# Seven modulation vectors: from dot products on VectorE to column-group matmuls on TensorE

## The chip, the core and the metric

The kernel runs on one core of a Trainium2 chip. The metric is device time in microseconds (us) of one execution, taken as the median of several; smaller is better. The engines that matter here are PE (TensorE, the matrix engine), DVE (VectorE), ACT (ScalarE), POOL (GpSimd) and SP (the queue that issues most of the DMAs). Each works through its own instructions in a fixed order.

## The reference, cut to what matters

A two-layer model handles 256 prompt tokens and 1024 sample tokens. Each layer has a mixer and an MLP, and each of these is modulated by six vectors of 1024 numbers per layer, made from a conditioning vector (one for the prompt, one for the sample):

```python
def _modulation(cvec, w, b):            # cvec (., 1024), w (1024, 6144), b (6144,)
    m = jax.nn.silu(cvec) @ w + b
    return jnp.split(m[:, None, :], N_MOD, axis=-1)

for l in range(DEPTH):                  # DEPTH = 2
    mp = _modulation(c_ctx[None, :], mod_w[l], mod_b[l])
    ms = _modulation(c, mod_w[l], mod_b[l])
    hp = _rmsnorm(xp, norm_mix[l]) * (1.0 + mp[1]) + mp[0]
    ...                                 # mixer; x = x + m[2] * mixer
    hp = _rmsnorm(xp, norm_mlp[l]) * (1.0 + mp[4]) + mp[3]
    xp = xp + mp[5] * _mlp(hp, mlp_w1[l], mlp_w2[l])
    ...                                 # the same for the sample stream with ms
```

Everything is float32. The MLP is `square(relu(h @ w1)) @ w2` with 4096 hidden units.

## The kernel before, in words

The activations stand as 8 tiles of 128 channels by 1280 tokens (`NT`). A float32 product is made of three matmuls on rounded halves (`fp32r`: high by high, high by low, low by high).

The program goes through filter preparation, the even mixer with attention, a first MLP, the odd mixer (Hyena and FNet), and a second MLP. It is written as a Python trace. The instructions of each engine are then put in order by a planner that runs through the trace with durations of its own (`schedule_with_timeline_sim=True`): what stands earlier in the program goes first where it is ready, and later work fills in. Tiles come from pools with a fixed number of buffers; a tile that finds no free buffer waits for the release of an earlier one.

`mlp` (L786 on) has two stages. Its first stage (`w1`) runs 16 turns (`for j in range(16)`), each of seven products of 24 matmuls in `product` (L846; two turns are begun ahead). The weights come by `wraw` (a DMA into `wr`, L811), `wset` (sums on POOL, L821 and the `sub` helper L300, through a temporary `s1`) and `wtile` (a rounding copy on ACT, L805, and a subtraction on DVE or POOL, L300). DVE and ACT take the products out of PSUM (L857, L860, L921 to L929), DVE squares the rectified results (L927, L930) and SP stores them (L928, L931). The second stage (`w2`) has its matmuls at L1034 and starts with PSUM reopened, after `drain(filler)`.

At the end of each turn `pull(filler, 4)` advances a generator by four steps. In the second MLP that generator is empty. In the first MLP it is `fill2`, which computes seven of the twelve modulation vectors: layer 0's sixth, and all six of layer 1. It does so with `modulation(l, which)`: for each vector, two halves of the input dimension and eight output chunks, a weight tile `mt` of 128 outputs by 512 inputs (256 KB) is loaded (L380), and for each of the two conditioning vectors DVE multiplies it with a broadcast copy `cb` of silu(c) and sums along the row (L382). `cb` comes from DRAM (`cscr`), written there by `silu_rows` between the two filter transforms. Partial sums lie in `macc` and are added up at L388 and L389.

The other five vectors (all of layer 0 but the sixth) are made by `modulation_pe`, three at the start and two inside attention: the conditioning vector stands as stationary weights (`silu`, 32 columns, two of them used), the weight tile `mw` streams 256 columns, and four input chunks go to four column groups of PE, so that each lands in 32 partitions of its own in one PSUM bank (L357). ACT copies the bank to `ms` (L362), and eight small matmuls with the selection matrix `sel` (L368) add the four groups and turn the result; DVE adds the bias (L369).

The temporaries `mt`, `mj`, `ms`, `s1` and several others share one pool (`tp`, tag `t`) of 4 buffers of 128 by 512 floats. `silu` takes one of the 24 large slots of pool `gp` (tag `g`) until attention is through. `tbank` gives one of two PSUM banks.

Of the kernel before, what the change touches and what calls it, by code (L numbers as in the profile page):

```python
# [8 lines left out]
F32 = mybir.dt.float32  # L9
F32R = mybir.dt.float32r  # L10
AF = mybir.ActivationFunctionType
ALU = mybir.AluOpType
# [131 lines left out]
def _pack(i):  # L144
    def A(x):
        return np.asarray(x)

    o = {}
# [3 lines left out]
    o["crow"] = np.stack([A(i["c_ctx"]), A(i["c"])[0]])  # L152
    mw = A(i["mod_w"])
    o["mw"] = mw[0, :, :5120].reshape(2, 4, 128, 20, 256).transpose(3, 0, 2, 1, 4).reshape(20, 2, 128, 1024)
    o["mt"] = mw.reshape(2, 2, 512, 6, 4, 2, 128).transpose(0, 3, 1, 4, 6, 5, 2).reshape(2, 6, 2, 4, 128, 1024)
# [40 lines left out]
    for t, n in enumerate(("lru_w_r", "lru_w_i")):  # L196
        w = A(i[n])[0]
# [26 lines left out]
def build(tc, a, out, dbg=None):  # L224
# [6 lines left out]
    tp = root.enter_context(tc.tile_pool(name="tp", bufs=4))  # L231
# [13 lines left out]
    def slot(name, shape, dt=F32, tag="g"):  # L245
        return gp.tile(shape, dt, tag=tag, name=name, bufs=SLOTS if tag == "g" else HSLOTS)

    def tmp(name, shape=(128, 512)):
        return tp.tile(list(shape), F32, tag="t", name=name)
# [9 lines left out]
    def tbank():  # L259
        return psum["t"].tile([128, 512], F32, tag="t", name="pt")  # L260
# [28 lines left out]
    cscr = dp.tile([2, 1024], F32, name="cscr")  # L289
# [29 lines left out]
    st = slot("silu", [128, 8, 32])  # L319
    mod = [[cp.tile([128, 8, 2], F32, name=f"mod{l}{i}") for i in range(6)] for l in range(2)]  # L320
    macc = cp.tile([128, 6, 2, 8, 2], F32, name="macc")
# [5 lines left out]

    def silu_rows():
        crow = slot("crow", [2, 1024])
        csg = slot("csg", [2, 1024])  # L330
        ld(crow, a["crow"])
        S.activation(csg, crow, AF.Sigmoid)
        V.tensor_tensor(csg, csg, crow, ALU.mult)
        ld(cscr, csg)

    def modulation_pe(i, bk=tbank, tags=("wr",)):
        mss = []
        for jj in range(2):
            ws = []
            for n in range(4):  # L340
# [5 lines left out]
                (ld if len(tags) == 1 else LDM)(w.rearrange("p k c -> p (k c)"), a["mw"][4 * i + 2 * jj + h, kk])  # L346
# [25 lines left out]
    def modulation(l, which):  # L372
        for hf in range(2):
            cb = cp.tile([128, 2, 512], F32, tag="cb", name="cb")
            for s_ in range(2):
                ld(cb[:, s_], cscr[s_:s_ + 1, 512 * hf:512 * hf + 512].to_broadcast([128, 512]))
            for i in which:
                for c in range(8):
                    w, j = tmp("mt"), tmp("mj")
                    ld(w, a["mt"][l, i, hf, c // 2, :, 512 * (c % 2):512 * (c % 2) + 512])  # L380
                    for s_ in range(2):
                        V.scalar_tensor_tensor(j if s_ == 0 else w, w, 1.0, cb[:, s_], ALU.mult, ALU.mult,  # L382
                                               accum_out=macc[:, i, hf, c, s_:s_ + 1])
                    if c % 2:
                        yield
        for i in which:
            m = mod[l][i]
            V.tensor_tensor(m, macc[:, i, 0], macc[:, i, 1], ALU.add)  # L388
            V.tensor_tensor(m, m, mb[:, l, 8 * i:8 * i + 8].unsqueeze(2).to_broadcast([128, 8, 2]), ALU.add)  # L389
        yield  # L390
# [1507 lines left out]
    # ================= program =================  # L1898
    with root:
# [74 lines left out]
        silu_rows()  # L1974
# [98 lines left out]
```

## Time and profile before

| | us |
|---|---|
| three runs: median (lowest to highest) | 3344.59 (3343.64 to 3347.43) |
| profiled execution, span from first to last instruction | 3345.9 |
| PE busy with matmuls in the span | 2960.5 (88%) |
| DVE busy | 2512.5 (75%) |
| POOL busy | 1406.4 (42%) |
| ACT busy | 1225.1 (37%) |

The page gives the span of the profiled execution and no other time of it; it lies 1.3 us above the median of the runs and inside their spread. A float32 matmul (not rounded halves) is recorded as two MATMUL instructions: L357 has 96 calls for three vectors and 192 records.

In the rows below, a group of instructions is given as line, engine, operation, output<-input, shapes, count, then busy time and mean duration, then the engine's idle time just before and what ended it. A timeline row is start, length, engine, line, operation and count, with the idle time before it in brackets. A wait row is who waited, for whom, total, times and longest.

### The profile page before, as it was taken

To read this page: it belongs to the slowest core of one execution; us is meant where nothing else is said; L and a number is where in the kernel's file an instruction comes from. 1 tells how busy PE (TensorE), PEld (TensorE's weight loads), DVE (VectorE), ACT (ScalarE), POOL (GpSimd) and SP (SyncE) were. 2 spreads that over 40 slices of the span, in tenths; PEclk is the share of its full clock that TensorE was granted. 3 is DMA by queue.
4 is the path that set the end of the run, shared out by engine and by line. 5 is a ranking of instruction groups with operands and counts; after the bars stand their busy time and mean duration, and the time that the engine had idled before them with its cause. 6 is when DMAs were issued, how large, how long until landed. Compare 5 with 4: busy or idle time off the path is not lost. (4 is left out here: it accounts for less than half of the span.)

```text
span 3345.9 us, 46730 instructions
## 1 busy us (share of the span) xinstructions
PE 2960.5 (88%) x18190; PEld 2716.9 (81%) x18190; DVE 2512.5 (75%) x3172; ACT 1225.1 (37%) x2032; POOL 1406.4 (42%) x912
## 2 busy tenths in 40 slices
PE   6799978897999998989799998887979999899977
PEld 3577767796988887989778876777979999898976
DVE  6886798648999987887983257875686656788896
ACT  5556757634111125333233332322432222533322
POOL 3530054524433336555630025543244344555563
PEclk8899989998999998999899998898989999999988
DMA  6363232341445443132331235546212223323232
GB/s 237 115 235 111 99 126 81 128 163 60 167 161 167 161 167 111 64 101 70 101 139 37 82 121 176 182 145 208 101 70 86 102 97 125 109 70 97 68 131 95
DMA packets 133336, 407.03 MB, mean 122 GB/s; under 512 B 14886, under 2 KB 29622, under 8 KB 133116
## 3 DMA queue, kind: packets, MB, share of 16 engines
q1 hardware_dynamic: 121596, 362.10, 31.6%
q0 software_dynamic: 11520, 41.95, 4.2%
q8 instruction: 144, 2.36, 0.3%
q14 instruction: 76, 0.62, 0.1%
HBM read 306.70 MB, written 97.29 MB: 121 GB/s over the span
## 5 line engine op out<-in xcount | busy, mean ns | idle before, releaser
L846 PE MATMUL pd<-BT,wt 128*128 128x320 f32 x3072 | 474.9, 314 | 42.5 <-ACT BT L764 21.6
L805 ACT CAST wt<-wr 128x512 fp32r<-128x512 f32 x360 | 221.2, 620 | 770.3 <-PE pd L1034 233.3
L846 PEld LDWEIGHTS pd<-BT,wt 128*128 128x128 f32 x3072 | 463.5, 192 | 48.1 <-ACT BT L764 22.6
L1034 PE MATMUL pd<-oT,wt 128*128 128x320 f32 x2688 | 427.8, 318 | 64.5 <-DVE acc L1040 54.5
L1034 PEld LDWEIGHTS pd<-oT,wt 128*128 128x128 f32 x2688 | 413.3, 195 | 72.7 <-issue 31.1
L846 PE MATMUL pd<-B,wt 128*128 128x320 f32 x2304 | 364.0, 315 | 35.2 <-DVE u L926 14.9
L846 PEld LDWEIGHTS pd<-B,wt 128*128 128x128 f32 x2304 | 349.4, 192 | 41.5 <-ACT wt L805 16.9
L1034 PE MATMUL pd<-o,wt 128*128 128x320 f32 x2016 | 324.7, 319 | 42.5 <-DVE acc L1040 25.8
L1034 PEld LDWEIGHTS pd<-o,wt 128*128 128x128 f32 x2016 | 310.5, 196 | 51.5 <-issue 24.6
L1040 DVE TENSOR_TENSOR acc<-acc,pd 128x640 f32<-128x640 f32 x336 | 270.2, 812 | 84.1 <-PE pd L1034 83.9
L300 DVE TENSOR_TENSOR wt<-wr,wt 128x512 fp32r<-128x512 f32 x276 | 265.8, 965 | 61.7 <-ACT wt L805 61.6
L923 POOL TENSOR_TENSOR u<-ut,u 128x640 f32<-128x640 f32 x32 | 55.0, 1719 | 413.0 <-ACT u L922 277.2
L300 POOL TENSOR_TENSOR ur<-ur 128x640 f32<-128x640 f32 x84 | 165.3, 1979 | 111.7 <-DVE o L300 69.5
L300 POOL TENSOR_TENSOR wt<-wr,wt 128x512 fp32r<-128x512 f32 x84 | 133.6, 1590 | 164.3 <-ACT wt L805 164.3
L300 POOL TENSOR_TENSOR wr<-wr 128x512 f32<-128x512 f32 x120 | 196.9, 1641 | 8.0
L692 PE MATMUL pb<-hh,wl 128*128 128x258 f32 (+1 forms) x720 | 191.9, 369 | 0.0
L692 PE MATMUL pb<-hh,wh 128*128 128x258 f32 (+1 forms) x720 | 191.5, 368 | 0.5 <-ACT hh L643 0.3
L692 PE MATMUL pb<-hl,wh 128*128 128x258 f32 (+1 forms) x720 | 191.5, 367 | 0.0
L303 ACT CAST wh<-wr 128x1024 fp32r<-128x1024 f32 x74 | 77.5, 1048 | 195.8 <-PE pd L692 79.8
L725 POOL TENSOR_TENSOR nacc<-nacc,nsq 128x640 f32<-128x640 f32 (+2 forms) x36 | 60.3, 1675 | 210.2 <-ACT nsq L724 210.1
L692 PEld LDWEIGHTS pb<-hh,wh 128*128 128x128 f32 x720 | 121.9, 190 | 27.9 <-issue 6.5
L692 PEld LDWEIGHTS pb<-hh,wl 128*128 128x128 f32 x720 | 121.9, 191 | 25.8 <-issue 6.0
(536 smaller groups left out, 6419.2 us busy)
## 6 DMA issues: line engine op xcount, KB each, us to landing
wr<-in_w_dram SPq DMA_DIRECT2D x136, 512.0 KB, 3.6
uscr<-u SPq DMA_DIRECT2D x64, 640.0 KB, 3.3
ur<-uscr SPq DMA_DIRECT2D x64, 640.0 KB, 4.9
tab<-in_dft_dram POOLq DMA_DIRECT2D x79, 512.0 KB, 4.7
mt<-in_mt_dram SPq DMA_DIRECT2D x112, 256.0 KB, 3.0
mw<-in_mw_dram SPq DMA_DIRECT2D x40, 512.0 KB, 4.7
x<-in_x_dram SPq DMA_DIRECT2D x16, 640.0 KB, 8.6
xmid<-x SPq DMA_DIRECT2D x32, 320.0 KB, 2.1
```

The costliest lines, as they stand in the source:

```text
L300: eng.tensor_tensor(o, x, y, ALU.subtract)
L303: S.copy(hi, src)
L692: T.matmul(ps[c][:, 0:N], w[wi][:, sl], hs[k][hi][:, c0:c0 + N], start=(ki == 0 and pi == 0), stop=(ki == nk - 1 and pi == 2))
L725: (V if last else G).tensor_tensor(s.acc[:, c0:c1], s.acc[:, c0:c1], sq, ALU.add)
L805: S.copy(t[:, 0], src)
L846: T.matmul(ps[:, c, 0:NQ], w[:, wi, 128 * k:128 * k + 128], B[n][k][:, hi_, NQ * c:NQ * c + NQ], start=(k == 0 and pi == 0), stop=(k == 3 ...
L923: G.tensor_tensor(u0[:, hi], t, u1[:, hi], ALU.add)
L1034: T.matmul(ps[:, z, 0:NQ], w[:, wi, sl], B2[n, k][:, hi_, NQ * z:NQ * z + NQ], start=(k == 0 and pi == 0), stop=(k == 1 and pi == 2))
L1040: V.tensor_tensor(d, d, ps[:, :, 0:NQ], ALU.add)
```

## The change

`modulation` no longer uses DVE dot products. Per vector it now runs eight steps; each loads two `mw` tiles of 256 KB and issues four float32 matmuls, one to each column group, with `silu` stationary. After each four steps ACT copies the bank to `ms`; after eight, eight `sel` matmuls and one DVE addition follow. A vector takes nine advances of the generator, seven take 63 of the 64 that the 16 turns give. The loads are as many and as large as before (112 of 256 KB). `silu_rows`, `cscr`, `crow`, `cb` and `macc` go. `silu` gets a buffer of its own that is never given back, and pool `tp` has 6 buffers in place of 4. `modulation_pe` keeps its code and reads the newly laid out array.

```diff
-    o["crow"] = np.stack([A(i["c_ctx"]), A(i["c"])[0]])
     mw = A(i["mod_w"])
-    o["mw"] = mw[0, :, :5120].reshape(2, 4, 128, 20, 256).transpose(3, 0, 2, 1, 4).reshape(20, 2, 128, 1024)
-    o["mt"] = mw.reshape(2, 2, 512, 6, 4, 2, 128).transpose(0, 3, 1, 4, 6, 5, 2).reshape(2, 6, 2, 4, 128, 1024)
+    o["mw"] = mw.reshape(2, 2, 4, 128, 24, 256).transpose(0, 4, 1, 3, 2, 5).reshape(2, 24, 2, 128, 1024)
...
-    tp = root.enter_context(tc.tile_pool(name="tp", bufs=4))
+    tp = root.enter_context(tc.tile_pool(name="tp", bufs=6))
...
-    st = slot("silu", [128, 8, 32])
+    st = cp.tile([128, 8, 32], F32, name="silu")
-    macc = cp.tile([128, 6, 2, 8, 2], F32, name="macc")
...
-    def silu_rows():
-        crow = slot("crow", [2, 1024])
-        csg = slot("csg", [2, 1024])
-        ld(crow, a["crow"])
-        S.activation(csg, crow, AF.Sigmoid)
-        V.tensor_tensor(csg, csg, crow, ALU.mult)
-        ld(cscr, csg)
...
     def modulation(l, which):
-        for hf in range(2):
-            cb = cp.tile([128, 2, 512], F32, tag="cb", name="cb")
-            for s_ in range(2):
-                ld(cb[:, s_], cscr[s_:s_ + 1, 512 * hf:512 * hf + 512].to_broadcast([128, 512]))
-            for i in which:
-                for c in range(8):
-                    w, j = tmp("mt"), tmp("mj")
-                    ld(w, a["mt"][l, i, hf, c // 2, :, 512 * (c % 2):512 * (c % 2) + 512])
-                    for s_ in range(2):
-                        V.scalar_tensor_tensor(j if s_ == 0 else w, w, 1.0, cb[:, s_], ALU.mult, ALU.mult,
-                                               accum_out=macc[:, i, hf, c, s_:s_ + 1])
-                    if c % 2:
+        for i in which:
+            mss = []
+            for jj in range(2):
+                ps = tbank()
+                for h in range(2):
+                    for kk in range(2):
+                        ws = []
+                        for z in range(2):
+                            w = tmp("mw", (128, 2, 256))
+                            ld(w.rearrange("p k c -> p (k c)"), a["mw"][l, 4 * i + 2 * jj + h, kk, :, 512 * z:512 * z + 512])
+                            ws.append(w)
+                        for g in range(4):
+                            T.matmul(ps[32 * g:32 * g + 32, 256 * h:256 * h + 256], st[:, 4 * kk + g, :], ws[g // 2][:, g % 2, :],
+                                     start=kk == 0, stop=kk == 1)
                         yield
-        for i in which:
-            m = mod[l][i]
-            V.tensor_tensor(m, macc[:, i, 0], macc[:, i, 1], ALU.add)
-            V.tensor_tensor(m, m, mb[:, l, 8 * i:8 * i + 8].unsqueeze(2).to_broadcast([128, 8, 2]), ALU.add)
-        yield
+                ms = tmp("ms")
+                S.copy(ms, ps)
+                mss.append(ms)
+            p2 = tbank()
+            for c in range(8):
+                T.matmul(p2[:, 2 * c:2 * c + 2], mss[c // 4][:, 128 * (c % 4):128 * (c % 4) + 128], sel, start=True, stop=True)
+            V.tensor_tensor(mod[l][i], p2[:, 0:16].rearrange("p (c s) -> p c s", s=2),
+                            mb[:, l, 8 * i:8 * i + 8].unsqueeze(2).to_broadcast([128, 8, 2]), ALU.add)
+            yield
...
         dft(fa, fa_fill)
-        silu_rows()
         dft(fb, fb_fill)
```

## Rows read from the trace of the kernel before

**Rows 1.** The page's busy time of each engine over the whole span.
```profile
span 3345.9 us, 46730 instructions
PE 2960.5 (88%) x18190; PEld 2716.9 (81%) x18190; DVE 2512.5 (75%) x3172; ACT 1225.1 (37%) x2032; POOL 1406.4 (42%) x912
```

**Rows 2.** Busy time by stretch (length; PE, PEld, DVE, ACT, POOL; PEclk, DMA, GB/s).
```profile
774.90:1261.60 486.70, 419.00 (x2703) 408.69 (x2702) 449.27 (x753) 109.91 (x189) 194.64 (x114) 0.95 0.45 148
2405.60:2846.70 441.10, 407.70 (x2703) 403.81 (x2701) 288.69 (x283) 112.91 (x190) 196.08 (x115) 0.96 0.26 93
...
2472.00:2840.00 368.00, 367.16 (x2494) 366.89 (x2492) 223.64 (x211) 83.64 (x136) 155.10 (x93) 1.00 0.29 104
```

**Rows 3.** Timeline of PE: first and last edges of the first stage, both MLPs.
```profile
774.86 6.32 PE L846 MATMUL pd<-B,wt 128*128 128x320 f32 x42
...
1261.61 9.51 PE L1034 MATMUL pd<-o,wt 128*128 128x320 f32 x48 [7.99 <-DVE u L929]
...
2405.56 6.32 PE L846 MATMUL pd<-B,wt 128*128 128x320 f32 x42
...
2467.24 0.56 PE L846 MATMUL pd<-B,wt 128*128 128x320 f32 x2 [2.98 <-ACT B L764]
2469.85 1.43 PE L846 MATMUL pd<-B,wt 128*128 128x320 f32 x4 [2.05 <-DVE B L769]
...
2846.75 8.89 PE L1034 MATMUL pd<-o,wt 128*128 128x320 f32 x48 [7.59 <-DVE u L929]
```

**Rows 4.** Timeline of PE: one turn of the first MLP, one of the second.
```profile
950.45 3.75 PE L846 MATMUL pd<-B,wt 128*128 128x320 f32 x24 [1.27 <-DVE u L926]
955.84 10.81 PE L846 MATMUL pd<-BT,wt 128*128 128x320 f32 x72 [1.64 <-DVE u L929]
...
978.88 3.75 PE L846 MATMUL pd<-B,wt 128*128 128x320 f32 x24 [1.67 <-DVE u L926]
...
2511.55 3.68 PE L846 MATMUL pd<-B,wt 128*128 128x320 f32 x24
...
2536.20 3.68 PE L846 MATMUL pd<-B,wt 128*128 128x320 f32 x24
```

**Rows 5.** Groups of instructions by form, first MLP: the dot products.
```profile
L382 DVE SCALAR_TENSOR_TENSOR mt<-mt,cb 128x512 f32<-128x512 f32 x111 | 109.6, 989 | 0.6
L382 DVE SCALAR_TENSOR_TENSOR mj<-mt,cb 128x512 f32<-128x512 f32 x110 | 102.9, 936 | 21.6 <-DMA mt<-in_mt_dram 21.6
```

**Rows 6.** Timeline of PE in attention and at the start: column-group matmuls and neighbours.
```profile
496.20 1.93 PE L357 MATMUL tps<-mw,silu 128*32 128x256 f32 x32
...
497.74 0.40 PE L357 MATMUL tps<-mw,silu 128*32 128x256 f32 x4
498.07 0.66 PE L1382 MATMUL tps<-c_ident,pr 128*128 128x128 f32 x4
...
28.52 0.38 PE L465 MATMUL pb<-hid,fsm 128*128 128x256 f32 x1
28.83 2.37 PE L357 MATMUL pt<-mw,silu 128*32 128x256 f32 x40
```

**Rows 7.** Timeline of PE in attention: one vector's selection matmuls, next instruction.
```profile
559.07 1.95 PE L368 MATMUL tps<-c_sel,ms 128*128 128x2 f32 x16 [0.17 <-ACT ptile L1382]
560.87 0.63 PE L1382 MATMUL tps<-c_ident,pr 128*128 128x128 f32 x4
```

**Rows 8.** Tile ms: its copies (min/median/max ns), and who waited for it.
```profile
L362 ACT COPY ms<-tps x4: 585/588/593, 498.3 to 619.3; 128x512 f32<-128x512 f32 x4
...
  PE pt L368: 3.7, 2
```

**Rows 9.** DMA issues (count, KB, median us to landing), and waits on them, first MLP.
```profile
mt<-in_mt_dram SPq DMA_DIRECT2D x112, 256.0 KB, 3.0
...
SPq L380 <- DVE mt L382: 160.3, 59, 7.7
...
DVE mj L382 <- DMA mt<-in_mt_dram: 21.6, 17, 1.9
```

**Rows 10.** Instructions on silu_rows' tile: when and how long (min/median/max ns).
```profile
L332 ACT ACTIVATE csg<-crow x1: 1062/1062/1062, 165.9 to 165.9; 2x1024 f32<-2x1024 f32 x1
L333 DVE TENSOR_TENSOR csg<-csg,crow x1: 1206/1206/1206, 170.2 to 170.2; 2x1024 f32<-2x1024 f32 x1
```

**Rows 11.** Who waited for whom: temporaries in the filters, PE for a load.
```profile
ACT win L517 <- DVE O L532: 11.5, 4, 5.2
...
PE pt L357 <- DMA mw<-in_mw_dram: 5.4, 1, 5.4
```

More of the change, by code (lines that the diff above doesn't have):

```diff
@@ L288, in build @@
     bscr = dp.tile([2, 8, 128], F32, name="bscr")
-    cscr = dp.tile([2, 1024], F32, name="cscr")
     qscr = dp.tile([4, 128, NT], F32, name="qscr")
@@ L345, in modulation_pe @@
                     w = wp.tile([128, 4, 256], F32, tag=tags[n % len(tags)], name="mw")
-                (ld if len(tags) == 1 else LDM)(w.rearrange("p k c -> p (k c)"), a["mw"][4 * i + 2 * jj + h, kk])
+                (ld if len(tags) == 1 else LDM)(w.rearrange("p k c -> p (k c)"), a["mw"][0, 4 * i + 2 * jj + h, kk])
                 ws.append(w)
```

## The prediction

> **What bounds the kernel now.** The page's busy shares come first [rows 1]: PE leads with 88%, DVE follows with 75%. That mean says little about the stage that is changed, so the next view is the busy time by stretch. The same first stage of the MLP runs twice, once with the seven vectors beside it and once with nothing beside it, and the two stretches [rows 2] run from the first L846 matmul to the first L1034 matmul of each MLP [rows 3]. With the vectors the stage takes 486.7 us and DVE is busy 449.3 of it; without them it takes 441.1 and DVE is busy 288.7. The matmuls are the same (2703 records each). So the dot products cost 45.6 us of time today, through DVE: it evacuates products late, and PE stands before the next product. The timeline shows it turn by turn [rows 4]: a turn takes 978.88 - 950.45 = 28.4 us in the first MLP, with stops that end on DVE's L926 and L929, and 2536.20 - 2511.55 = 24.65 us in the second, without a stop. In the second, PE is busy 367.2 of 368 us [rows 2]. This is the fact on which the sum turns: once DVE is out of the way, PE is full, and whatever the new matmuls take on PE is paid in time.
>
> **What is removed.** The dot products are 111 and 110 instructions of 989 and 936 ns in that stretch [rows 5], about 212 us of DVE. All that they can give back in this stage is the difference to the stage that has none: -45.6 us. Nothing is late next but PE itself, which the second MLP shows.
>
> **What is added on PE.** The same operation exists already in attention [rows 6]. A burst of 32 records (16 calls, half a vector) starts at 496.20 and the next matmul starts at 498.07: 1.87 us. Seven vectors are 14 such halves: 14 x 1.87 = +26.2 us. Inside the burst a group of four columns starts every (497.74 - 496.20) / 7 = 0.22 us, so the four groups do run side by side; this is no matter of doubt. The selection matmuls of one vector occupy 559.07 to 560.87 [rows 7], 1.80 us; seven vectors: +12.6 us.
>
> The halves will not stand together as in attention. A generator step is only four calls (two groups of four columns), and steps wait for their loads. Each burst has two edges. From the last L465 matmul (256 columns, like a group's) to the first group it is 28.83 - 28.52 = 0.31 us, and from the last group to the next other matmul 498.07 - 497.74 = 0.33 [rows 6]; less the spacing of 0.22 that is 0.09 and 0.11, so 0.20 a burst. There are at least 16 bursts (the four steps of a turn together) and at most 56 (each step alone), and 7 of selection. I take two a turn, 32: 39 x 0.20 = 7.8, less the 14 exits of 0.11 that the halves above already hold (1.5): +6.3 us, bounds +3.1 and +11.1. The edges next to an L846 matmul are not in the trace; these are the nearest rows. Sum on PE: 26.2 + 12.6 + 6.3 = +45.1 us, bounds 41.9 and 49.9. So the gain of 45.6 is spent on PE almost to the microsecond.
>
> A rule bears on the edges: the Trainium skill, TensorEngine Tiling, Key Properties, says that changing the tiling mode drains TensorE. The rows show edges of 0.09 and 0.11 us where a group's own record lasts 0.40, so they bear out a cost but not a full wait: by a full one (0.40 - 0.22 = 0.18 at each edge, 39 x 0.36 = 14.0 in place of 7.8) the forecast would come 6 us later.
>
> **What lies in gaps.** PE is not quite full at the ends of the stage. In the second MLP it stands 2.98 and 2.05 us before the turns settle, and 7.59 us before the second stage [rows 3]. The first loads were issued at about that early place, and the last steps fall at the end, so some new matmuls lie there free: bounds 0 and -12.6 us. I take -4: two steps or so early, a selection at the end, since the last copy and selection chain also has to clear its PSUM before the second stage may open all banks.
>
> **The waits that are added.** First, PE now waits for the `mw` loads. They are the same number and size on the same queue as `mt` (112, 256 KB, median 3.0 us to landing) [rows 9], and each needs a buffer that an earlier step on PE releases, where it was DVE before; SP stood 160.3 us on that. Behind a waiting load on SP stand the weight loads L811 and the stores L928 and L931; behind a waiting matmul on PE stand the next turn's products, and DVE, ACT and SP after them. Before, the engine that used the loads stood 21.6 us for them in 17 stops [rows 9], with a load taking two of four buffers. Now it takes one of six, so more lie ahead, but `s1` and `ms` share them and a turn's four steps want eight. Bounds 0 and +21.6; I take +8, about a third, because the buffers are deeper. At the start of the kernel PE stood once, 5.4 us, for the same kind of load [rows 11].
>
> Second, the selection waits for ACT's copy to `ms`, 14 copies of 0.59 us [rows 8]. ACT is busy only 113 of 441 us in the stage [rows 2], and the selection comes a generator step later. At the start two of three vectors cost PE 3.7 us together [rows 8]. Bounds 0 and 7 x 1.85 = +13; I take +1. Behind a waiting copy on ACT stand the weight casts L805, which the next product needs.
>
> Third, `tbank` alternates two banks among sums and selection; the copies that release them are those just counted, so nothing more is added. DVE's bias addition (seven times, in place of fourteen additions) is hidden beside DVE's free third of the stage.
>
> **Elsewhere.** `silu_rows` goes: 1.06 us of ACT and 1.21 us of DVE near 170 us [rows 10], and a few small transfers on SP: -1 us, bounds 0 and -2. The two more buffers of `tp` are seen by the filters' `win` too, where ACT stood 11.5 us for a release [rows 11]; ACT is not the bound there, and the freed slot of `silu` is of the same kind: I take 0. The planner may order other stages a little differently with either; a price stands nowhere, and I bound it at 5 us both ways by that same stop, halved.
>
> **How the numbers follow.** -45.6 + 45.1 - 4 + 8 + 1 - 1 = +3.5 us. The profiled span (3345.9) is 1.3 us above the median of the runs, so the difference is put on the median: 3344.6 + 3.5 = 3348 us. What a measurement of this kernel can tell from no change is about 0.2%, 6.7 us, that is 3337.9 to 3351.3.
>
> Case A, an even swap of DVE's stops for PE's work: 3348, own range 3338 to 3357. Chance 0.45.
>
> Rival B, faster: the loads are always there before PE comes, steps run together, and the gaps take 8 us: -45.6 + 41.9 - 8 - 1 = -12.7, so 3332. For it: deeper buffers, and PE stands for transfers hardly anywhere in this trace. Against it: a turn's four steps want more buffers than there are. Chance 0.25.
>
> Rival C, slower: PE waits on landings. In each of 16 turns at least one load can start only when a matmul of the same turn has released its buffer; if its landing of 3.0 us is exposed on PE at half, that is 16 x 1.5 = 24 in place of the 8 above, and with the copies to `ms` adding 6 instead of 1 it gives 3344.6 + 3.5 + 16 + 5 = 3369. Fully exposed it is 3393. It decides from the point where PE stands over 0.7 us a turn for loads (11 us in all, 3 above the sum). For it: the 17 stops before, with a mean of 1.27 us [rows 9]. Against it: the planner puts other products between. Chance 0.30.
>
> From these: faster by over 0.2%: 0.22 of B and 0.02 of A; within: 0.37 of A, 0.03 of B, 0.02 of C; slower: 0.28 of C and 0.06 of A. So 0.24, 0.42, 0.34. The range reaches half way into both rivals: 3331 to 3374.
>
> **What would show it.** In the changed kernel the dot products are gone and DVE's busy time in the stage falls by about 210 us; the stops before L926 and L929 vanish. The stage from the first L846 to the first L1034 matmul should last about 490 us, with PE nearly full: that is the swap. If it lasts about 475, B holds; if it is over 500 and PE's waits name `mw` or `ms`, C. The column-group line should take some 26 us and the selection 12.6 of PE's time between products. The prediction is wrong in its base if the stage with an empty generator is not what is left when DVE is relieved, or if the other stages move by more than a few microseconds.

## The result: 28 us slower, with PE full and DVE free

| | before | after |
|---|---|---|
| median of four runs, us | 3344.32 (3343.64 to 3347.43) | 3372.64 (3372.1 to 3373.01) |
| span of the profiled execution, us | 3345.9 | 3370.3 |
| before the first product of the first MLP, us | 774.9 | 777.9 |
| first stage of the first MLP, us | 486.7 | 509.8 |
| all behind it, us | 2084.3 | 2082.6 |

The ratio is 1.0084 (1.0069 to 1.0098). Of the 24.4 us between the two profiled executions 23.1 lie in the stage that was changed. The medians lie 28.3 apart. Most of the other 4 us come from the profiled execution of before: by its span it is the slowest of the four runs (3347.43), 3.1 above their median. The prediction set its span of 3345.9 beside the runs' median and found 1.3 us; a run's time is longer than its span (here 3372.1 and 3370.3). Since the prediction put its difference on the median, nothing follows from that.

Line numbers shift by six: the product L846 of before is L840, the second stage L1034 is L1028. The new column groups are L373, their copy L377, the selection L381, the load L370. The page's busy shares of after, which answer to [rows 1]:

```profile
span 3370.3 us, 47355 instructions
...
PE 3017.5 (90%) x18750; PEld 2733.8 (81%) x18750; DVE 2351.1 (70%) x2716; ACT 1234.0 (37%) x2044; POOL 1398.7 (42%) x912
...
mw<-in_mw_dram SPq DMA_DIRECT2D x112, 256.0 KB, 4.4
```

DVE lost 161 us and PE gained 57. The last row answers to the first of [rows 9]: the same 112 loads, now 4.4 us to landing where `mt` had 3.0. Busy time by stretch in after, the first and the second MLP's first stage, with the columns of [rows 2]:

```profile
777.90:1287.70 509.80, 479.53 (x3263) 429.77 (x3261) 291.85 (x299) 121.48 (x205) 197.81 (x116) 0.97 0.41 140
2429.00:2870.00 441.00, 407.43 (x2708) 403.54 (x2706) 287.07 (x284) 113.44 (x191) 195.31 (x115) 0.96 0.26 93
```

DVE fell from 449 to 292 us, as low as in the MLP that has no vectors, and PE is busy 479.5 of 509.8. So the swap took place as described: PE no longer stops for DVE's evacuations, and PE is the bound. It was not an even swap, because PE took more than was given back. Groups of instructions of after in that stage (busy time counts a moment once, however many of the group run in it; then the mean of one in ns, then idle time ahead):

```profile
L373 PE MATMUL pt<-mw,silu 128*32 128x256 f32 x448 | 52.1, 395 | 0.5 <-DMA mw<-in_mw_dram 0.5
L381 PE MATMUL pt<-c_sel,ms 128*128 128x2 f32 x112 | 13.6, 247 | 0.0
```

The selection is where the prediction had it (12.6). The column groups occupy 52.1 us where it had 26.2, and they waited for a load only 0.5 us. Timeline of PE in part of one turn of after (start, length, operation, count):

```profile
992.36 0.63 PE L373 MATMUL pt<-mw,silu 128*32 128x256 f32 x4
992.91 0.55 PE L840 MATMUL pd<-B,wt 128*128 128x320 f32 x2
993.40 0.63 PE L373 MATMUL pt<-mw,silu 128*32 128x256 f32 x4
993.95 0.71 PE L840 MATMUL pd<-B,wt 128*128 128x320 f32 x3
994.59 0.63 PE L373 MATMUL pt<-mw,silu 128*32 128x256 f32 x4
995.15 0.71 PE L840 MATMUL pd<-B,wt 128*128 128x320 f32 x3
995.79 0.63 PE L373 MATMUL pt<-mw,silu 128*32 128x256 f32 x4
996.34 1.30 PE L840 MATMUL pd<-B,wt 128*128 128x320 f32 x7
997.48 10.73 PE L840 MATMUL pd<-BT,wt 128*128 128x320 f32 x72
1008.05 1.19 PE L840 MATMUL pd<-B,wt 128*128 128x320 f32 x7
```

Here is what the prediction had not thought of. A step is four calls, one to each column group, so eight records. The bursts of 4 records are **half a step**: two column groups run, the other two are idle, and the second half of the step comes some products later. One such half costs as much as a whole step. From 994.59 to 995.79 it is 1.20 us for one burst and three products; products alone start every (1008.05 - 997.48) / 72 = 0.147 us, so the burst costs 1.20 - 3 x 0.147 = 0.76 us. A burst of a whole step follows below in e2_four and costs 0.77.

In this stage PE leaves the products 74 times for new matmuls and comes back; 70 of these bursts hold column groups, four hold the selection alone. 53 of the 70 are half steps, and five larger ones (of 12 or 20 records) hold an odd half each, which costs in full too: from its start to the next product a burst of 12 records takes 0.99 us (at 848.76), one of 16 takes 1.00 (at 867.54). The time from one product's start to the next one's, less 0.147, summed over these 74, is 66.0 us.

### The profile page after: what moved, and what is told of

Its sections match the earlier page's. It is cut to its first block, busy times and chain, and to the rows that moved or that the text cites. A ratio compares the mean times of both kernels' runs of the same rounds, so it can differ in the third digit from the quotient of the medians.

```text
span 3370.3 us, 47355 instructions
## 1 busy us (share of the span) xinstructions
PE 3017.5 (90%) x18750; PEld 2733.8 (81%) x18750; DVE 2351.1 (70%) x2716; ACT 1234.0 (37%) x2044; POOL 1398.7 (42%) x912
## 5 line engine op out<-in xcount | busy, mean ns | idle before, releaser
L840 PE MATMUL pd<-BT,wt 128*128 128x320 f32 x3072 | 472.8, 313 | 32.8 <-ACT BT L758 22.0
L840 PEld LDWEIGHTS pd<-BT,wt 128*128 128x128 f32 x3072 | 461.5, 191 | 38.1 <-ACT BT L758 23.1
L1028 PE MATMUL pd<-oT,wt 128*128 128x320 f32 x2688 | 426.5, 318 | 60.9 <-DVE acc L1034 54.4
L1028 PEld LDWEIGHTS pd<-oT,wt 128*128 128x128 f32 x2688 | 412.1, 195 | 69.1 <-issue 31.0
L297 DVE TENSOR_TENSOR wt<-wr,wt 128x512 fp32r<-128x512 f32 x276 | 297.0, 1078 | 144.8 <-ACT wt L799 144.7
L840 PE MATMUL pd<-B,wt 128*128 128x320 f32 x2304 | 371.1, 315 | 8.8 <-DVE B L763 4.5
L840 PEld LDWEIGHTS pd<-B,wt 128*128 128x128 f32 x2304 | 344.6, 190 | 36.5 <-issue 21.8
L1028 PE MATMUL pd<-o,wt 128*128 128x320 f32 x2016 | 324.9, 319 | 42.6 <-DVE acc L1034 27.5
L1028 PEld LDWEIGHTS pd<-o,wt 128*128 128x128 f32 x2016 | 310.5, 196 | 51.5 <-issue 26.1
L1034 DVE TENSOR_TENSOR acc<-acc,pd 128x640 f32<-128x640 f32 x336 | 270.2, 813 | 84.0 <-PE pd L1028 84.0
L686 PEld LDWEIGHTS pb<-hl,wh 128*128 128x128 f32 x720 | 122.3, 190 | 25.7 <-issue 5.8
```

Of the source, the lines that this page charges most:

```text
L297: eng.tensor_tensor(o, x, y, ALU.subtract)
L686: T.matmul(ps[c][:, 0:N], w[wi][:, sl], hs[k][hi][:, c0:c0 + N], start=(ki == 0 and pi == 0), stop=(ki == nk - 1 and pi == 2))
L840: T.matmul(ps[:, c, 0:NQ], w[:, wi, 128 * k:128 * k + 128], B[n][k][:, hi_, NQ * c:NQ * c + NQ], start=(k == 0 and pi == 0), stop=(k == 3 ...
L1028: T.matmul(ps[:, z, 0:NQ], w[:, wi, sl], B2[n, k][:, hi_, NQ * z:NQ * z + NQ], start=(k == 0 and pi == 0), stop=(k == 1 and pi == 2))
L1034: V.tensor_tensor(d, d, ps[:, :, 0:NQ], ALU.add)
```

## The experiments

Two theories stood after the result. **H, half-filled bursts**: the two loads of a step land apart by the planner's reckoning, and since it orders single matmuls and not steps, it starts the two groups whose tile is there, alone; the price is the idle half of the array and twice the number of edges. **W, waits**, the prediction's rival C: PE or its weight queue stands for landings of `mw`, which the page's 4.4 us make longer, and the trace puts some of that down to PE as busy.

Every kernel ran beside a run of the kernel before on the same chip: 3346.84 for the first four, 3339.98 for the next four, 3344.99 (the median of 13 runs) for the last two. Each of the first eight kernels ran once, and the 13 runs of before reach from 3342.35 to 3349.32, so the argument goes by the stage and not by the whole time. How far a stage varies by itself is shown by the second MLP's first stage, which no kernel here changes: 439.6 to 442.0 us in all twelve traces. By the stage is meant the stretch from the first product to the first second-stage matmul of the first MLP.

**e1_none.** The base alone: the seven vectors' sums are left out, so this kernel computes something else, and only the bias reaches `mod`.

```diff
-            yield from modulation(0, (5,))
-            yield from modulation(1, (1, 0, 2, 4, 3, 5))
+            for l, i in ((0, 5), (1, 1), (1, 0), (1, 2), (1, 4), (1, 3), (1, 5)):
+                V.tensor_copy(mod[l][i], mb[:, l, 8 * i:8 * i + 8].unsqueeze(2).to_broadcast([128, 8, 2]))
+            yield
```

> The changed kernel with the seven vectors left out of the first MLP: their sums are not computed, each is only its bias. This is the base of the sum. If relieving the first MLP of all seven leaves the stage that the second MLP shows, the stage from its first product to the second stage's first matmul takes 441 us and the kernel 3344.3 - 45.6 = 3299 us. If the first MLP is longer than the second for another reason than the vectors, the stage stays clearly above 441 (at 450 or more) and the kernel above 3308, and then the base of the prediction was wrong and not the price of the new matmuls.

Measured 3308.54 us. Its stage by stretch:

```profile
781.50:1222.00 440.50, 406.65 (x2703) 402.68 (x2702) 287.34 (x287) 112.94 (x190) 196.59 (x115) 0.96 0.26 93
```

440.5 us, so the base of the sum was right: what the dot products cost in the stage before was 486.7 - 440.5 = 46.2 us, and what their replacement costs in after is 509.8 - 440.5 = 69.3. The whole kernel came out later than the 3299 forecast, mainly since its first product starts at 781.5 instead of 774.9. The planner put some instructions ahead of it in another order; whether that is the cause is not shown (see what stays open).

**e2_four.** The four matmuls of a step are tied one behind the other, beginning with the tile that lands last, so no half of a step can run alone. Nothing else changes.

```diff
-                        for g in range(4):
-                            T.matmul(ps[32 * g:32 * g + 32, 256 * h:256 * h + 256], st[:, 4 * kk + g, :], ws[g // 2][:, g % 2, :],
-                                     start=kk == 0, stop=kk == 1)
+                        prev = None
+                        for g in (2, 3, 0, 1):
+                            with (tc.issue_after(prev) if prev is not None else contextlib.nullcontext()):
+                                prev = T.matmul(ps[32 * g:32 * g + 32, 256 * h:256 * h + 256], st[:, 4 * kk + g, :],
+                                                ws[g // 2][:, g % 2, :], start=kk == 0, stop=kk == 1).ins
```

> The changed kernel, but the four matmuls of a step are tied in a row, those of the later load first, so that all four column groups start together. Theory H (half-filled bursts): in the changed kernel 53 of 70 bursts hold only two of four column groups and cost 0.65 us each, as much as a burst of four groups (0.66); tied, 53 become about 27, so 53 x 0.65 - 27 x 0.66 = 17 us less: 3355, stage 493. Rival W (waits for loads: the stage is long because PE or the queues stand for landings and buffers): a step now waits for the later of its two loads, so the time is the same or longer, 3372 or more.

Measured 3352.1 us, 20.5 below after. Its column groups and stage, by group and by stretch:

```profile
L375 PE MATMUL pt<-mw,silu 128*32 128x256 f32 x448 | 34.2, 393 | 0.8 <-DMA mw<-in_mw_dram 0.8
...
774.90:1264.60 489.70, 458.25 (x3264) 425.30 (x3262) 292.43 (x299) 121.72 (x205) 198.03 (x116) 0.96 0.43 146
```

The same 448 records occupy PE 34.2 us instead of 52.1, and PE waits for loads 0.8 us although every burst now needs both tiles. The 53 half steps are gone and 49 bursts are left of 74, and the stage is 20.1 us shorter. This speaks for H and against W, by which a burst that needs both tiles waits longer. One whole step in its timeline of PE:

```profile
897.29 0.64 PE L375 MATMUL pt<-mw,silu 128*32 128x256 f32 x8
897.86 1.16 PE L842 MATMUL pd<-B,wt 128*128 128x320 f32 x6
898.94 0.64 PE L375 MATMUL pt<-mw,silu 128*32 128x256 f32 x8
```

898.94 - 897.29 - 6 x 0.147 = 0.77 us for 8 records, beside 0.76 for 4 in after.

**e3_pair.** Two steps in one chain: four tiles are loaded, then eight matmuls follow each other.

```diff
+                    prev = None
+                    for kk in (1, 0):
+                        for g in (2, 3, 0, 1):
+                            with (tc.issue_after(prev) if prev is not None else contextlib.nullcontext()):
+                                prev = T.matmul(ps[32 * g:32 * g + 32, 256 * h:256 * h + 256], st[:, 4 * kk + g, :],
+                                                ws[2 * kk + g // 2][:, g % 2, :], start=kk == 1, stop=kk == 0).ins
+                    yield
```

> As e2_four, but two steps (four loads, eight calls) are tied into one burst. Theory H with a fixed price of about 0.22 us for the two edges of a burst: 28 bursts of 4 x 0.216 + 0.22 = 1.09 in place of 56 of 0.66 at most, 6 us less than e2_four, 3349. Rival W: four of the six buffers are held until one burst is done, so landings move onto PE and it is slower than e2_four.

Measured 3344.15 us, another 8.0 less, of which 5.4 lie in the stage:

```profile
774.10:1258.40 484.30, 452.96 (x3264) 427.12 (x3262) 292.14 (x299) 121.36 (x205) 198.06 (x116) 0.96 0.44 148
...
917.77 1.07 PE L378 MATMUL pt<-mw,silu 128*32 128x256 f32 x16
918.77 7.30 PE L845 MATMUL pd<-B,wt 128*128 128x320 f32 x48
925.91 0.31 PE L845 MATMUL pd<-BT,wt 128*128 128x320 f32 x1
926.15 1.07 PE L378 MATMUL pt<-mw,silu 128*32 128x256 f32 x16
```

The upper row is by stretch, the others are PE's timeline. Its expectation had 6 us for the stage. From 917.77 to 926.15, less 49 products, 16 records cost 8.38 - 7.20 = 1.18 us. Two steps apart cost 1.54, so the pair saves one set of edges, 0.36. With 33 bursts the change is about even with before (3346.84 on that chip); this is the swap that the prediction described, and 3348 is what it had for it.

**e4_noload.** Two tiles are loaded once and used by all seven vectors; the other loads are left out, so its sums are not the right ones. `tp` has 4 buffers. No matmul can be parted from its neighbour by a load.

```diff
-                        ws = []
-                        for z in range(2):
-                            w = tmp("mw", (128, 2, 256))
-                            ld(w.rearrange("p k c -> p (k c)"), a["mw"][l, 4 * i + 2 * jj + h, kk, :, 512 * z:512 * z + 512])
-                            ws.append(w)
+                        if not mwf:
+                            for z in range(2):
+                                w = cp.tile([128, 2, 256], F32, name=f"mwf{z}")
+                                ld(w.rearrange("p k c -> p (k c)"), a["mw"][l, 4 * i + 2 * jj + h, kk, :, 512 * z:512 * z + 512])
+                                mwf.append(w)
+                        ws = mwf
```

> The changed kernel with its 112 loads in the first MLP left out but two: every step multiplies with the same two tiles, which stay (the vectors are wrong by that), and the pool of temporaries has four buffers again. Theory H in its full form (the split comes from two loads that land apart): all steps come whole, in bursts of a turn or so; 112 x 0.216 + 16 x 0.22 + 12.6 + 7 x 0.2 = 42 us over the bare stage, 483, kernel about 3342. If instead the planner splits the steps for another reason, two-group bursts stay and the time stays near 3370. Rival W: also about 3342, but then the timeline of the changed kernel should have shown PE standing idle before its column-group matmuls, and e2_four should not be faster.

Measured 3346.85 us, with a stage of 480.5. Groups of PE, and one burst in its timeline:

```profile
L376 PE MATMUL pt<-mwf,silu 128*32 128x256 f32 x448 | 28.1, 383 | 0.0
...
920.19 1.93 PE L376 MATMUL pt<-mwf,silu 128*32 128x256 f32 x32
922.05 7.31 PE L843 MATMUL pd<-B,wt 128*128 128x320 f32 x48
```

Without loads there is no half step: the groups stand in 19 bursts, seven of them of 32 records, and occupy 28.1 us. The burst is that of attention [rows 6]: 922.05 - 920.19 = 1.86, there 1.87. So it is the loads that part the steps. What their transfers as such cost is not separated: with them, e3_pair's stage is only 3.8 us longer, but 64 of the 448 records of e4_noload lie at the start of the stage, where PE stands otherwise, and its stage ends 13.7 us behind the last product instead of 9.9. The whole kernel is not faster than e3_pair for another reason, 780.6 us ahead of the first product instead of 774.1.

**e5_tp4.** Only the buffers of `tp` go back to 4. By H loads land further apart and more steps split; by W PE waits.

```diff
-    tp = root.enter_context(tc.tile_pool(name="tp", bufs=6))
+    tp = root.enter_context(tc.tile_pool(name="tp", bufs=4))
```

> The changed kernel with 4 buffers in the pool of temporaries in place of 6, nothing else. It tells what the two added buffers are worth. Theory H: with one step's loads ahead at most, no turn begins with several steps ready, so nearly all bursts hold two groups: up to 112 of 0.65 us in place of the present mix, up to 73 + 14 = 87 us over the bare stage in place of 66, kernel 3372 to 3393, and PE still without waits for loads. Rival W: PE stands for landings, shown as waits of the column-group line, and the time grows by more than 30 us.

Measured 3386.9 us, the slowest of all, where before took 3339.98 on the same chip. Its group, its stage and PE's waits (total, times, longest):

```profile
L373 PE MATMUL pt<-mw,silu 128*32 128x256 f32 x448 | 61.0, 399 | 4.1 <-DMA mw<-in_mw_dram 4.1
...
777.90:1307.10 529.20, 492.19 (x3264) 431.76 (x3262) 299.76 (x305) 124.28 (x210) 203.80 (x119) 0.96 0.41 137
...
PE pt L373 <- DMA mw<-in_mw_dram: 4.1, 2, 3.6
```

The stage is 19.4 us longer than in after. 72 bursts are half steps and PE's groups occupy 8.9 us more; waits for loads grew by 3.6. Nearly all of that is one wait of 3.65 us behind the last product, and the end of the stage, from the last product to the second stage, grew from 9.9 to 18.1. So of the 19.4 us some 9 lie in the bursts and 8 at the end, where a late load is part of it: each theory has a share here, and H had forecast no wait. The two more buffers that the change brought were worth keeping.

**Variants.** If PE's time is paid in full in this stage, the vectors belong where PE has room, or partly back on DVE. **v1_late** keeps e3_pair's form, leaves three vectors in the first MLP and moves four beside the Hyena steps.

```diff
-            yield from modulation(1, (1, 0, 2, 4, 3, 5))
+            yield from modulation(1, (1, 0))
...
+        m1 = modulation(1, (2, 4, 3, 5))
+
+        def beside(g):
+            for _ in g:
+                pull(m1, 3)
+                yield
+        h0 = beside(hyena(0, vt, Y))
```

> A version: only three vectors (the MLP's own and the two that the next norm needs) stay in the first MLP, in bursts of two tied steps; the four that are needed after the odd mixer are made beside the Hyena convolutions, where PE stands 67 of 700 us. Three vectors cost 3 x (4 x 1.09 + 2.1) = 19 us in the first MLP: stage 460. The other four cost 26 us of PE; wholly in gaps the kernel takes 3344.3 - 45.6 + 19 = 3318, wholly on the path 3344; I expect about 3330. If gaps in the odd mixer are no longer than a wait's chain lets them be, nothing is gained there and it is 3340 or more.

Measured 3333.59 us beside 3339.98 of before. The stage fell to 458.8; the stretch from the second stage of the first MLP to the second MLP grew from 1143.9 to 1157.2. The kernels that have no vector in that stretch take between 1134.3 and 1145.1 us for it, so four vectors cost 12 to 23 us there, 3 to 6 each, where three in the first MLP cost 18.3, 6.1 each. The whole gain, one run against one, is no larger than the 6.7 us that a measurement can't tell from no change.

**v2_dve3_late4** puts the three vectors of the first MLP back on DVE, in the old code with 4 buffers, and the other four beside Hyena in the form of e2_four.

> A version: the three early vectors stay dot products on VectorE in the first MLP (as in the kernel before), the four late ones are column-group matmuls (four tied) beside the Hyena convolutions. It also asks how the price of dot products grows: seven cost 45.6 us. If it is in proportion, three cost 19.5 and the stage takes 461; if it is the overload that costs, since DVE then has 289 + 3 x 30 = 380 of 441 us to do, three cost about 5 and the stage takes 446. The four late ones cost 29 us of PE, of which about half should lie in gaps: 3344.3 - 45.6 + 5 to 20 + 15 = 3319 to 3333.

Measured 3337.36 us, above the range expected. The stage takes 459.7, so three vectors on DVE cost 19.2 of the 46.2 that seven cost, about in proportion. All of it lies in the first seven turns, since the generator is pulled four steps a turn. PE's timeline in them has the stops of [rows 4]:

```profile
926.46 3.75 PE L874 MATMUL pd<-B,wt 128*128 128x320 f32 x24 [1.34 <-DVE u L954]
931.85 10.81 PE L874 MATMUL pd<-BT,wt 128*128 128x320 f32 x72 [1.64 <-DVE u L957]
...
954.43 3.75 PE L874 MATMUL pd<-B,wt 128*128 128x320 f32 x24 [1.20 <-DVE u L954]
```

Such a turn lasts 954.43 - 926.46 = 28.0 us; the later ones, with no dot products in them, last 24.6.

**v3_split** keeps both in the first MLP: three vectors on DVE and four on PE, their steps spread evenly over the 64 advances.

```diff
+            for k in range(64):
+                if k * 36 // 64 != (k - 1) * 36 // 64:
+                    pull(p)
+                if k * 27 // 64 != (k - 1) * 27 // 64:
+                    pull(d)
+                yield
```

> A version: all seven in the first MLP, three as dot products on VectorE and four as tied column-group matmuls, side by side. PE: 4 x (8 x 0.66 + 2.1) = 29.5; VectorE: 5 (overload) to 20 (in proportion). Stage 441 + 35 to 50 = 476 to 491, kernel 3334 to 3348.

Measured 3330.09 us. The stage takes 475.8, 35.3 over the base: 29.6 lie in PE's 35 bursts, 5.1 at its end (13.0 instead of 7.9), so little is left for DVE's three vectors, though its turns, lengthened by PE's bursts, give DVE more time. The whole time is below the range expected because the stretch behind the stage, which holds none of the vectors, took 1134.3 us instead of 1143.9. That asks for them spaced and alone, which is **v4_spread3**: v2_dve3_late4 with its 27 steps spread over the 64 advances.

```diff
-        xt = mlp(0, xt, n1, fill2(), n2)
+
+        def spaced():
+            d = fill2()
+            for k in range(64):
+                if k * 27 // 64 != (k - 1) * 27 // 64:
+                    pull(d)
+                yield
+            drain(d)
+        xt = mlp(0, xt, n1, spaced(), n2)
```

> v2_dve3_late4 with one change: the dot-product steps of the three early vectors are spaced evenly over the 16 turns instead of four a turn in the first seven. If DVE's price is one of crowding within a turn (in v2 the three vectors cost 459.7 - 440.6 = 19 us in seven turns, in v3 about 5 when spread), the stage takes about 445 and the kernel 14 us less than v2, about 3323. If the price goes by the number of dot products, the stage stays near 460 and the kernel near 3337.

Measured 3323.61 us (3319.18 to 3327.55, four runs) beside 3344.99 of before: ratio 0.9931 (0.9914 to 0.9947). It is the fastest kernel here that computes everything. Its stage by stretch, and a turn in its timeline:

```profile
777.30:1225.70 448.40, 409.97 (x2704) 404.09 (x2702) 365.05 (x483) 112.99 (x190) 193.85 (x115) 0.96 0.36 123
...
945.34 7.19 PE L874 MATMUL pd<-B,wt 128*128 128x320 f32 x48
969.98 7.19 PE L874 MATMUL pd<-B,wt 128*128 128x320 f32 x48
```

The same three vectors now cost 7.9 us instead of 19.2. The turn shown holds five dot products and takes 24.64 us, as long as one that has none. From the fourth turn on, the eight turns with four to seven dot products take 24.64 or 24.65 us; the four with eight take 24.85 to 25.87. Over half of the 7.9 us lie ahead of the fourth turn. **v5_spread4** adds a fourth vector to DVE in the same way (35 steps over 64 advances) and leaves three beside Hyena.

> As v4, with four vectors as spaced dot products in the first MLP and three column-group vectors beside the Hyena convolutions. Crowding: a turn has 24.65 us, DVE 16 of them without the vectors, and four vectors add 4 x 30 / 16 = 7.5: 23.5, still under the turn but with little room, so 5 to 12 us in the stage; the odd mixer gives back one of four vectors' price there (15 us for four), 4 us. Kernel 3318 to 3327. If it costs by number, 26 us in the stage and about 3340.

Measured 3340.9 us (3334.31 to 3347.11, ten runs), ratio 0.9985 (0.9975 to 0.9994). Its stage takes 466.6:

```profile
780.10:1246.70 466.60, 415.09 (x2704) 407.56 (x2703) 380.29 (x549) 111.81 (x189) 191.30 (x114) 0.95 0.37 127
...
PE pd L874 <- DVE u L954: 7.2, 3, 2.7
```

The four vectors cost 26 us where three cost 8. That is what the expectation had for a price by number (26, and 3340), and not what it had for crowding. Some 6 us of it may be this execution, the slowest of the ten. The price can't go by the number alone, since the same 96 dot products cost 19.2 and 7.9. But neither does it go by how many fall in a turn: in v5_spread4 a turn with six lasts 29.1 us and one with eleven 24.9.

The traces show one way in which it comes about. DVE works in a fixed order: where a dot product waits for its load, the evacuation behind it waits too. First v5_spread4, then v4_spread3 at the same place:

```profile
1075.50 1.21 DVE L382 SCALAR_TENSOR_TENSOR mj<-mt,cb 128x512 f32<-128x512 f32 x1 [2.40 <-DMA mt<-in_mt_dram]
1083.70 0.81 DVE L954 TENSOR_TENSOR u<-u,pd 128x640 f32<-128x640 f32 x1
1084.66 5.26 PE L874 MATMUL pd<-B,wt 128*128 128x320 f32 x24 [2.73 <-DVE u L954]
```
```profile
1037.81 1.22 DVE L382 SCALAR_TENSOR_TENSOR mj<-mt,cb 128x512 f32<-128x512 f32 x1 [0.53 <-DMA mt<-in_mt_dram]
1046.04 0.81 DVE L954 TENSOR_TENSOR u<-u,pd 128x640 f32<-128x640 f32 x1
```

From the dot product to the evacuation it is 8.2 us in both. DVE's three longest waits ahead of L954 (2.52, 2.40 and 2.04 us) each end in a stop of PE of 2.5 to 2.7 us; shorter ones, up to 1.88 us, end in none in either kernel, with one exception (a stop of 2.0 us at 900.90 behind a wait of 0.57). Over the stage DVE stands 20.2 us for `mt` here and 9.3 in v4_spread3. Why the loads land later here was not followed up, and these stops are only part of the 18 us between the two kernels.

## Why the prediction was wrong, and its range right by luck

The forecast was an even swap at 3348, inside a range of 3331 to 3374 that was wide enough to hold the numbers of both rivals. The measured 3372.64 lies inside it by luck: 1.4 us below its upper end and near the number of rival C (3369), for a reason that is not C's and that the prediction did not have. It had given 0.34 to a kernel that is slower by more than a measurement can tell from no change, and 0.42 to no such difference. Its steps against the two profiled executions, in us:

| step | predicted | measured | from |
|---|---|---|---|
| DVE's stops go | -45.6 | -46.2 | stage of e1_none |
| column groups, four side by side | +24.7 | +24.2 | 112 sets of four at 0.216 |
| half the groups idle | not in the sum | +12.5 | 58 halves at 0.216 |
| selection | +12.6 | +12.6 | 112 records at 0.1125, busy 13.6 |
| edges of bursts | +7.8 (39 at 0.20) | +21.0 (70 at 0.30) | what is left of PE's 70.3 |
| gaps and waits | +5 (-4 + 8 + 1) | -0.8 | standing -2.8, end of stage +2.0 |
| elsewhere | -1 | +1.3 | ahead +3.0, behind -1.7 |
| sum | +3.5 | +24.6 | spans: +24.4 |

PE's 70.3 are the 62.1 that lie in the bursts (66.0 less the 3.9 by which two early bursts, in which PE stood, are longer than others of 8 records) and 8.2 in the product behind each: it is followed by its neighbour after 0.25 us and not 0.147, so 0.11 late, 74 times. The 3.0 us ahead are no effect of the change that is shown (see what stays open).

**What held.** The base: without the vectors the first MLP's stage is that of the second (440.5 and 441.0), and relieved of DVE's stops PE is full, so new work on PE is paid in time. The four groups run side by side, at the spacing read in attention. The selection costs what its row said. DVE's busy time fell by 157 us where the prediction said about 210, because its other work took longer with the dot products gone. The casts of the weights in that stage show it, first in before, then in after (groups of DVE):

```profile
L300 DVE TENSOR_TENSOR wt<-wr,wt 128x512 fp32r<-128x512 f32 x94 | 74.4, 793 | 0.6 <-ACT wt L805 0.5
```
```profile
L297 DVE TENSOR_TENSOR wt<-wr,wt 128x512 fp32r<-128x512 f32 x94 | 106.8, 1137 | 84.7 <-ACT wt L799 84.6
```

The same 94 casts take 793 ns each beside the dot products and 1137 without them, 32 us more in all. DVE has the room for it (84.7 us of idle time ahead of them), so nothing is the later for it. The trace shows which casts are slow: in after 51 of the 94 run beside no POOL instruction for more than a tenth of their length and take 0.68 to 0.69 us; the other 43 take 1.67 on average. In before 74 of the 94 had no POOL instruction beside them. The second MLP in [rows 2] would have given the right figure: 449.3 - 288.7 = 160.6.

**The step that failed** is "I take two a turn, 32", with the bound "at most 56 (each step alone)". The prediction held a step of four calls to be one thing. It has two loads, and a matmul depends on its own tile alone, so a step can come in two bursts: 112, not 56, is the upper end, and 70 bursts with column groups came, where the prediction took 32. The same error hides a second term. A burst of two groups leaves the other half of the array idle and lasts as long as one of four (0.76 and 0.77), so the price per record doubles; the price of 1.87 for half a vector was read in attention, where 32 records stand together [rows 6]. Four steps cost 8 x 0.76 = 6.1 us when all are split, 4 x 0.77 = 3.1 in e2_four, 2 x 1.18 = 2.4 in e3_pair. The sentence "the four groups do run side by side; this is no matter of doubt" was true of the rows and taken too far: it holds for calls that are issued together.

**The edge** was read too low as well: 0.20, measured 0.30, and in a burst's own cycle 0.76 - 2 x 0.216 = 0.33. The prediction counted the way in and the way out to the next matmul's start, and not that the matmul behind it is late too. It had worked out a second figure, 0.36 by a full wait at both edges. The runs are nearer to that than to the 0.20 that was taken; for the 39 bursts assumed it would have meant only 6 us. The Trainium skill, TensorEngine Tiling (Array Packing), Key Properties, says that changing the tiling mode drains TensorE. The trace agrees in so far as only the column groups pay: a burst of selection alone, whose matmuls fill the array as the products do, has next to no edge. PE's timeline of after:

```profile
1083.37 0.90 PE L840 MATMUL pd<-BT,wt 128*128 128x320 f32 x5
1084.10 0.95 PE L381 MATMUL pt<-c_sel,ms 128*128 128x2 f32 x8
1084.91 5.38 PE L840 MATMUL pd<-BT,wt 128*128 128x320 f32 x35
```

The five products start 0.73 / 5 = 0.147 us apart, and the eight selection matmuls occupy 0.81, 0.89 with the 0.08 by which the second product behind them is late; 8 x 0.1125 is 0.90. So the 7 x 0.20 that the prediction had for selection edges were not there.

**Waits** fell out in the other direction. The sum gave loads 8 us and `ms` 1. PE waited for `mw` once, 0.5 us, and for `ms` not at all. SP's largest wait for a buffer in after's stage, which answers to [rows 9]:

```profile
SPq L370 <- PE pt L373: 12.1, 16, 2.3
```

SP stands 12.1 us for PE where it stood 160.3 for DVE, so loads go out early and a landing of 4.4 us doesn't show. It stands 16 times, as often as C reckoned, but PE has other products meanwhile. Rival C had the bound "if it is over 500 and PE's waits name `mw` or `ms`": the first half came, the second did not, and that was the test that told them apart. What the prediction held against C, that "the planner puts other products between", is true: it hides the landings, and it also cuts the bursts.

**Gaps.** The prediction gave them 4 us. PE does stand 2.8 us less than in e1_none, but the last vector's copy, selection and addition come behind the last product, and the second stage starts 9.9 us after it instead of 7.9. PE's timeline of after at that place:

```profile
1278.10 1.07 PE L373 MATMUL pt<-mw,silu 128*32 128x256 f32 x16
1279.10 1.95 PE L381 MATMUL pt<-c_sel,ms 128*128 128x2 f32 x16
1287.74 4.63 PE L1028 MATMUL pd<-o,wt 128*128 128x320 f32 x16 [6.69 <-DVE mod L382]
```

The wait that was DVE's `u` [rows 3] is now DVE's `mod`, as the clause about the copy and selection chain feared.

**What stays open.** The time ahead of the first product lies between 774.1 and 781.5 us among these kernels, with no edit there but buffers and what follows. About half of that is no matter of the program: after, e2_four, e3_pair and v1_late run the same instructions in the same order on PE, DVE, ACT and POOL up to there, and the product starts at 777.9, 774.9, 774.1 and 774.2. The rest was read, not explained. The whole is as large as what a measurement of this kernel can tell from no change, and somewhat more than the 5 us at which the prediction bounded the planner's order.

## What to carry to other kernels

A matmul that uses a quarter of the array is worth its price only in the company of the other three: before counting a burst, look which load each call waits for, and tie the calls together where a planner may part them. Count what enters and leaves a burst three times, on the way in, on the way out and in the matmul behind it, and count bursts by the smallest thing that can stand alone. Work on an engine off the critical path has no fixed price: the same dot products cost 19.2 us in one place and 7.9 in another, and one vector more cost 18. Read what stands behind each piece in its engine's order, and how late its loads may land.

## What the runs showed of the hardware that was not expected

- Two column groups alone cost the same as all four: 0.76 and 0.77 us with their edges; each further set of four records costs 0.21 (1.18 - 0.77 = 0.41 for two).
- A change between float32 column groups and the rounded products costs 0.30 to 0.33 us a burst, of which 0.11 falls on the product behind it. A burst of selection matmuls on the whole array has no such cost beside its own 8 x 0.1125.
- The same 256 KB loads on the same queue had a median of 4.4 us to landing in after and 3.0 in before, and PE was hardly the later for it (0.5 us). What lengthens them was not tested.
- The same DVE casts took 793 ns each beside the dot products and 1137 without them. Those beside no POOL instruction took 0.68 to 0.69 us in both, the other 43 in after 1.67 on average. No run tested POOL as the cause.
- Three vectors of dot products on DVE cost 19.2 us crowded into seven turns and 7.9 spread over sixteen; a fourth cost 18 more, part of it by evacuations that stood behind a dot product's load.
